# HGRN2's level steps in two-bank score tiles ahead of the projections, its outputs between the attention's units, and the output projection's rows in that order

## The chip, the cores and the metric

The kernel runs on one core of a Trainium2 chip. Its engines work from queues of their own: TensorE (PE in the profile; PEld is its weight load), VectorE (DVE), ScalarE (ACT), GpSimd (POOL) and SyncE (SP), which issues the DMAs here. Semaphores order them against each other. The metric is the device time of one execution in microseconds.

## The reference

One inference step of a two-layer backbone on 384 tokens: 128 context tokens (x_prompt) and 256 latent ones (x_sample), D = 1024, all in fp32. Layer 0 is the one that matters here: windowed attention (A) and a bidirectional HGRN2 (B) share one input projection and one output projection.

```python
def mixer_ab(h, w_in, w_out, sink, lb, gnorm, rope=None, ctx=None):
    qa, ka, va, qb, ib, ff, fb, gb = jnp.split(h @ w_in, EVEN_SPLIT, axis=-1)
    ...
    qb = jax.nn.silu(qb)...
    logf_f, kf = hgrn2_gate(ff, lb[0])      # f = lb + (1-lb)*sigmoid(z); log f, k = 1-f
    logf_b, kb = hgrn2_gate(fb, lb[1])
    ...
    oa = banded_gqa_with_context(rope(qa), rope(ka), va, k_ctx, v_ctx, sink)   # dense_gqa for context
    ob, s_f, s_b = hgrn2_bidir(qb, kf, logf_f, kb, logf_b, ib, s0_f, s0_b)
    ob = rms_norm(ob, gnorm) * jax.nn.silu(gb)
    y = jnp.concatenate([oa, ob], axis=-1) @ w_out
```

HGRN2 is, per head, a state S of 128 x 128 with S <- diag(f_t) S + k_t v_t and output q_t S_t, once forward and once backward, the two added. After the mixer comes x <- LN(alpha*x + gate*y), then a SwiGLU feed-forward; layer 1 (other mixers) follows, and nothing of it is touched.

## The kernel before

A scheduler sets the order of each engine's queue: instructions are taken by the order in which the program writes them, moved by a priority offset. `ahead(part)` sets that offset from the table `AHEAD` for what is written inside it, larger meaning earlier.

*Matmuls.* Activations and weights are split into a high and a low part (hH, hL; wh, wl), and `mm3` (L127 to L129) makes three matmuls of each product. `wload` (L118 to L123) loads a weight into one of three `wr` buffers with a DMA on SP, casts it to wh on ACT (L122) and subtracts on VectorE to get wl (L123). `proj_tm` gives tokens on partitions (tile pj), `proj_fm` features (pf).

*HGRN2.* Four heads in two pairs; a pair has 2 x 384 columns. `hg_proj(pr)` projects q and the two gates f. `hg_levels` builds the matrix AT of decayed scores within 128-token blocks: six diagonal blocks, then seven levels, level lv joining neighbours of m = 2^lv tokens. In each level ACT copies the halves of the scaled keys and queries (Fk, Bk, Fq, Bq) into Kc and Qc (L890 to L893), TensorE makes six score blocks hs (L872) into the one lv bank, four and then two, VectorE merges them into AT under a mask (L911), multiplies the four arrays by products of gates (L900), and forms the next products nB (L907, L908). `hg_out(pr)` then makes states and outputs: transposes tk, products up with the values vB, outputs ho, an rms norm (POOL's rsqrt, L110), the gate gB, transposes ty, and writes rows 4 + 2 pr and 5 + 2 pr of hH and hL.

*Attention.* `attention` is a generator of six steps: the context unit, four pairs of heads, and a last step; step n makes scores and softmax of a unit (s, pr) and then transposes and values of the unit before (pt, ov), which go into rows 0 to 3 of hH and hL.

*Output projection.* `out_first` (in the mixer) projects the first four rows that `ORDER` names onto columns 0 to 511 (o0, o1, o2); `boundary`, written after the mixer, loads the first rows' other columns (out_second, into pools `bndw`), gate gb (L477), x (L480), and the last four rows of w_out, and ends in LN. SP takes its DMAs in the order of its queue, so one that waits holds the rest.

*PSUM.* `open_psum(3, 3, 1)`: three banks for ps (s, pt, tk, up, ho, ty ...), three for pj, one for lv, beside psa's one.

Of the kernel before, what the change touches and what calls it, by code (L numbers as in the profile page):

```python
# [29 lines left out]
AHEAD = {"w": 1500, "w0": -700, "lv0": -30, "lv1": 0, "attA": 400, "attC": 400, "attD": 100, "fin": 500, "qs": -1500,  # L30
         "ada": -400, "ada_step": -500, "of0": -500, "of1": 1500, "ho0": -100, "ho1": -30, "gb": 100, "ib": -60,
# [6 lines left out]
ORDER = ((0, 1, 2, 3, 4, 5, 6, 7), (4, 5, 6, 7, 0, 1, 2, 3))  # L38
# [3 lines left out]
def tile_backbone_step(ctx, tc, I, O):  # L42
# [18 lines left out]
    def lvt(name):  # L61
        return psum["lv"].tile([P, 512], F32, tag="lv", name=name)
# [755 lines left out]
    def mixer_ab():  # L818
# [4 lines left out]
        M = Slots(es, {"one": (1, 0), "pr": (4, 768), "pt": (6, 512), "qS": (2, 1536), "qf": (3, 768),  # L823
                       "X": (8, 768), "at": (2, 768), "vB": (2, 768), "kq": (3, 768), "t2": (5, 512),
# [4 lines left out]
        def hg_tiles():  # L829
            return M.tile("qf", F32), [M.tile("X", F32) for _ in range(4)], [M.tile("qf", F32) for _ in range(2)]  # L830
# [9 lines left out]
        def ev_f(pr, d, X, f):  # L840
            def ev(j, acc):
# [687 lines left out]
```

## Time and profile before

| | us |
|---|---|
| median of three runs | 1096.12 |
| lowest and highest | 1095.95, 1098.69 |
| the profiled execution | 1095.94 |
| its span | 1094.1 |
| TensorE busy in it | 1036.0 |
| VectorE, ACT, POOL busy | 660.6, 440.8, 120.0 |

The span is what the profiler recorded of one execution; what is left of its time lies around it. A row of a timeline gives start and length; one of a group gives busy time, mean of one, and the idle time of the engine before them with what ended it. "hs<-kq" is the operation that writes hs and reads kq; a full-fp32 matmul leaves two records.

### The profile page before, as it was taken

The numbers are of one execution on the slowest core, as the hardware profiler recorded it, in microseconds if no ns is written. First come the engines' busy times: TensorE is split into PE (matmuls) and PEld (weight loads), VectorE is DVE, ScalarE is ACT, GpSimd is POOL, SyncE is SP. The second block draws the span as 40 slices with busy tenths as digits, with TensorE's granted clock in tenths as the row PEclk, the third lists the DMA queues.
The fourth block names the chain that finished last, engine by engine and source line by source line (L and its number), as shares of the span: only waits on it lengthen the run. The fifth ranks groups of instructions, "written<-read, shape, count | busy, mean of one in ns | idle before, by whom it ended". The sixth has DMA issues, their size and how long they took to land. (4 is left out here: it accounts for less than half of the span.)

```text
span 1094.1 us, 15881 instructions
## 1 busy us (share of the span) xinstructions
PE 1036.0 (95%) x6105; PEld 870.7 (80%) x6105; DVE 660.6 (60%) x1140; ACT 440.8 (40%) x804; POOL 120.0 (11%) x166
## 2 busy tenths in 40 slices
PE   5999999987999999999999998979899999999996
PEld 4788767555889999897778786666589999998885
DVE  2575855686598458458236875765489464443237
ACT  2365645363253323232223547545254333332231
POOL 0021201101110000000000343213130000000004
PEclk8999999997999999999999999989999999999998
DMA  9874243484047776766655431144126555543431
GB/s 305 258 222 124 86 142 123 140 275 164 23 150 219 249 221 219 232 210 214 237 190 159 152 108 45 35 150 165 47 79 194 151 172 153 159 135 116 135 116 58
DMA packets 114354, 173.13 MB, mean 158 GB/s; under 512 B 9419, under 2 KB 82150, under 8 KB 114278
## 3 DMA queue, kind: packets, MB, share of 16 engines
q1 hardware_dynamic: 113526, 171.78, 50.0%
q8 instruction: 48, 0.79, 0.3%
q10 hardware_dynamic: 752, 0.34, 0.1%
q14 instruction: 28, 0.23, 0.1%
HBM read 167.84 MB, written 4.24 MB: 157 GB/s over the span
## 5 line engine op out<-in xcount | busy, mean ns | idle before, releaser
L123 DVE TENSOR_TENSOR wl<-wr,wh 128x1024 fp32r<-128x1024 f32 (+4 forms) x200 | 235.7, 1182 | 234.9 <-ACT wh L122 232.3
L122 ACT ACTIVATE wh<-wr 128x1024 fp32r<-128x1024 f32 (+4 forms) x200 | 202.4, 1015 | 347.3 <-PE pf L128 124.0
L127 PE MATMUL pf<-hH,wh 128*128 128x384 f32 x688 | 232.7, 338 | 0.0
L129 PE MATMUL pf<-hH,wl 128*128 128x384 f32 x688 | 232.7, 338 | 0.0
L128 PE MATMUL pf<-hL,wh 128*128 128x384 f32 x688 | 232.6, 338 | 0.0
L129 PEld LDWEIGHTS pf<-hH,wl 128*128 128x128 f32 x688 | 129.4, 188 | 3.1 <-issue 3.1
L128 PEld LDWEIGHTS pf<-hL,wh 128*128 128x128 f32 x688 | 129.4, 188 | 2.7 <-issue 2.6
L127 PEld LDWEIGHTS pf<-hH,wh 128*128 128x128 f32 x688 | 129.4, 188 | 2.3 <-issue 2.2
L128 PE MATMUL o<-wl,aH 128*128 128x512 f32 (+1 forms) x280 | 101.2, 361 | 0.7 <-DVE wl L123 0.7
L127 PE MATMUL o<-wh,aH 128*128 128x512 f32 (+1 forms) x280 | 101.3, 362 | 0.4 <-DVE a L1175 0.4
L129 PE MATMUL o<-wh,aL 128*128 128x512 f32 (+1 forms) x280 | 101.0, 361 | 0.0
L129 PE MATMUL pj<-wh,hL 128*128 128x512 f32 (+3 forms) x240 | 89.0, 371 | 2.0 <-POOL hL L344 1.8
L127 PE MATMUL pj<-wh,hH 128*128 128x512 f32 (+3 forms) x240 | 89.2, 377 | 0.3 <-ACT vA L1106 0.2
L261 DVE SCALAR_TENSOR_TENSOR part<-ar,cT,part 128x512 f32<-128x512 f32 x112 | 80.2, 744 | 15.3 <-DMA ar<-in_w_ada 15.2
L128 PE MATMUL pj<-wl,hH 128*128 128x512 f32 (+3 forms) x240 | 89.0, 371 | 0.0
L110 POOL TENSOR_TENSOR ve<-ve,nhalf 128x1 f32<-128x1 f32 x12 | 7.0, 583 | 617.7 <-DVE ve L530 336.1
L127 PEld LDWEIGHTS o<-wh,aH 128*128 128x128 f32 x280 | 52.9, 189 | 10.2 <-issue 1.4
L128 PEld LDWEIGHTS o<-wl,aH 128*128 128x128 f32 x280 | 52.9, 189 | 9.0 <-DVE wl L123 1.0
L129 PEld LDWEIGHTS o<-wh,aL 128*128 128x128 f32 x280 | 52.8, 188 | 9.2 <-issue 1.2
L129 PEld LDWEIGHTS pj<-wh,hL 128*128 128x128 f32 x240 | 45.1, 188 | 12.2 <-POOL hL L344 2.7
L127 PEld LDWEIGHTS pj<-wh,hH 128*128 128x128 f32 x240 | 44.8, 188 | 10.4 <-issue 2.7
L128 PEld LDWEIGHTS pj<-wl,hH 128*128 128x128 f32 x240 | 45.1, 188 | 8.6 <-issue 1.4
(318 smaller groups left out, 1542.7 us busy)
## 6 DMA issues: line engine op xcount, KB each, us to landing
ar<-in_w_ada SPq DMA_DIRECT2D x80, 512.0 KB
wr<-in_w_ffn_down SPq DMA_DIRECT2D x44, 512.0 KB
wr<-in_w_ffn_gate SPq DMA_DIRECT2D x40, 512.0 KB
wr<-in_w_ffn_up SPq DMA_DIRECT2D x40, 512.0 KB
wr<-in_w_in_ab SPq DMA_DIRECT2D x18, 512.0 KB
ar<-in_w_ada SPq DMA_DIRECT2D x32, 256.0 KB
wr<-in_w_out SPq DMA_DIRECT2D x16, 512.0 KB
wr<-in_w_in_ab SPq DMA_DIRECT2D x16, 256.0 KB
```

What stands on the lines that cost most here:

```text
L110: nc.gpsimd.tensor_tensor(out=out, in0=v, in1=nhalf[:, :n], op=ALU.pow)
L122: nc.scalar.activation(hi, raw, AF.Copy)
L123: nc.vector.tensor_tensor(out=lo, in0=raw, in1=hi.bitcast(F32), op=ALU.subtract)
L127: nc.tensor.matmul(out, lh, rh, start=start, stop=False)
L128: nc.tensor.matmul(out, lh, rl, start=False, stop=False)
L129: nc.tensor.matmul(out, ll, rh, start=False, stop=stop)
L261: nc.vector.scalar_tensor_tensor(out=dst, in0=raw[:, j], scalar=sc, in1=dst, op0=ALU.mult, op1=ALU.add)
```

## The change

It touches five things. The tiles: a pair's keys are one tile X[0] (Fk, Bk), its queries another (Bq, Fq), f is one tile for both directions, so one access covers both halves. `hg_levels`: all six score blocks in one tile of two banks, one merge of 768 columns, one product for the keys, one nB, two copies on ACT. PSUM: `open_psum(2, 3, 1)`, where lv's one buffer now has two banks and ps has two. The program's order: hg_proj(1) and both hg_levels stand before the attention's projections, with new offsets. And the attention's six steps are split, three, then hg_out(0), one, out_first, one, hg_out(1), one, with `ORDER[0]` taking rows 2 and 3 last.

```diff
-AHEAD = {"w": 1500, "w0": -700, "lv0": -30, "lv1": 0, "attA": 400, "attC": 400, "attD": 100, "fin": 500, "qs": -1500,
-         "ada": -400, "ada_step": -500, "of0": -500, "of1": 1500, "ho0": -100, "ho1": -30, "gb": 100, "ib": -60,
+AHEAD = {"w": 1500, "w0": -700, "lv0": 1000, "lv1": 800, "attA": 400, "attC": 400, "attD": 100, "fin": 500, "qs": -1500,
+         "ada": -400, "ada_step": -500, "of0": -500, "of1": 1500, "ho0": 300, "ho1": 300, "gb": 100, "ib": -60,
-ORDER = ((0, 1, 2, 3, 4, 5, 6, 7), (4, 5, 6, 7, 0, 1, 2, 3))
+ORDER = ((0, 1, 4, 5, 6, 7, 2, 3), (4, 5, 6, 7, 0, 1, 2, 3))
...
-        return psum["lv"].tile([P, 512], F32, tag="lv", name=name)
+        return psum["lv"].tile([P, 2, 512], F32, tag="lv", name=name)
...
-        M = Slots(es, {"one": (1, 0), "pr": (4, 768), "pt": (6, 512), "qS": (2, 1536), "qf": (3, 768),
-                       "X": (8, 768), "at": (2, 768), "vB": (2, 768), "kq": (3, 768), "t2": (5, 512),
+        M = Slots(es, {"one": (1, 0), "pr": (4, 768), "pt": (6, 512), "qS": (2, 1536), "f": (1, 1536),
+                       "X": (4, 1664), "at": (2, 768), "vB": (2, 768), "kq": (3, 768), "t2": (5, 512),
...
+        def mixed(X, m):
+            v = X[:, 0:2 * (N2 + m)].rearrange("p (h r) -> p h r", h=2)[:, :, 0:N2]
+            return v.rearrange("p h (g a i) -> p h g a i", a=2, i=m)[:, :, :, 0, :]
...
             def scores(Kc, Qc, take):
-                for b0, nb in ((0, 4), (4, 2)):
-                    pp = lvt("hs").rearrange("p (b t) -> p b t", b=4)
-                    for b in range(nb):
-                        bs = slice((b0 + b) * P, (b0 + b + 1) * P)
-                        nc.tensor.matmul(pp[:, b, :], Kc[:, bs], Qc[:, bs], start=True, stop=True)
-                    take(pp[:, 0:nb, :], slice(b0, b0 + nb), nb)
+                pp = lvt("hs").rearrange("p a (b t) -> p (a b) t", b=4)
+                for b in range(6):
+                    nc.tensor.matmul(pp[:, b, :], Kc(b), Qc(b), start=True, stop=True)
+                take(pp[:, 0:6, :])
...
-                nc.scalar.activation(V(Qc)[:, :, 1, :], V(Fq)[:, :, 1, :], AF.Copy)
-                nc.scalar.activation(V(Qc)[:, :, 0, :], V(Bq)[:, :, 0, :], AF.Copy)
-                nc.scalar.activation(V(Kc)[:, :, 0, :], V(Fk)[:, :, 0, :], AF.Copy)
-                nc.scalar.activation(V(Kc)[:, :, 1, :], V(Bk)[:, :, 1, :], AF.Copy)
+                for c, x in ((Kc, Km), (Qc, Qm)):
+                    nc.scalar.activation(c.rearrange("p (g h i) -> p g h i", h=2, i=m),
+                                         x.rearrange("p h g i -> p g h i"), AF.Copy)
+                scores(blk(Kc), blk(Qc), merge)
...
-                for eng, T, hh, fac in ((nc.vector, Fk, 0, bf[:, :, 1]), (nc.vector, Bk, 1, bb[:, :, 0]),
-                                        (nc.vector, Fq, 1, bf[:, :, 0]), (nc.vector, Bq, 0, bb[:, :, 1])):
-                    eng.tensor_tensor(out=V(T)[:, :, hh, :], in0=V(T)[:, :, hh, :], in1=bc(fac), op=ALU.mult)
+                nc.vector.tensor_tensor(out=Km, in0=Km, in1=bc(kf), op=ALU.mult)
+                nc.vector.tensor_tensor(out=Qm[:, 1], in0=Qm[:, 1], in1=bc(bv[:, 0, :, 0]), op=ALU.mult)
+                nc.vector.tensor_tensor(out=Qm[:, 0], in0=Qm[:, 0], in1=bc(bv[:, 1, :, 1]), op=ALU.mult)
...
-                nc.vector.tensor_tensor(out=nf, in0=bf[:, :, 0], in1=bf[:, :, 1], op=ALU.mult)
-                nc.vector.tensor_tensor(out=nb_, in0=bb[:, :, 0], in1=bb[:, :, 1], op=ALU.mult)
+                nc.vector.tensor_tensor(out=nB, in0=bv[:, :, :, 0], in1=bv[:, :, :, 1], op=ALU.mult)
...
-        ps1 = open_psum(3, 3, 1)
+        ps1 = open_psum(2, 3, 1)
...
         lv0, lv1 = [], []
+        st1 = hg_proj(1)
+        with ahead("lv0"):
+            drain(hg_levels(*st0, lv0))
+        with ahead("lv1"):
+            drain(hg_levels(*st1, lv1))
         a_ctx()
         proj_tm(w, 512, 256, evac_kv)
         proj_tm(w, 0, 512, evac_q)
-        with ahead("lv0"):
-            drain(hg_levels(*st0, lv0))
-        st1 = hg_proj(1)
...
-        with ahead("lv1"):
-            drain(hg_levels(*st1, lv1))
-        with ahead("attA"):
-            drain(attention(M, Att(s_sample, s_prompt, lambda tl, h: vA[:, tl, h // 4, :], 0, SC_A, True)))
+        att = attention(M, Att(s_sample, s_prompt, lambda tl, h: vA[:, tl, h // 4, :], 0, SC_A, True))
+
+        def att_some(n):
+            with ahead("attA"):
+                for _ in range(n):
+                    next(att)
+
+        att_some(3)
         with ahead("ho0"):
             hg_out(0, st0[1], *lv0, vB[0])(gB[:, 0])
+        att_some(1)
         with ahead("of0"):
             first = out_first(I["w_out"][0], ORDER[0])
+        att_some(1)
         with ahead("ho1"):
             hg_out(1, st1[1], *lv1, vB[1])(gB[:, 1])
+        att_some(1)
```

Three places show what moves. First, TensorE's queue around pair 0's first scores (hs). Before (qf is the query of pair 0, pj0 and pj1 accumulators of a projection onto tokens, tk transposes a cached key):

```order
L127 MATMUL pj1_1094<-wh_1083,hH_89 128x512
L128 MATMUL pj1_1094<-wl_1084,hH_89 128x512
L129 MATMUL pj1_1094<-wh_1083,hL_90 128x512
L127 MATMUL pj1_1094<-wh_1110,hH_89 128x512
L872 MATMUL hs_1219<-qf_141,kq_1217 128x128 x4
L794 MATMUL tk_1051<-ident_75,t2_1049 128x128 x2
L128 MATMUL pj0_1087<-wl_1111,hH_89 128x512
L129 MATMUL pj0_1087<-wh_1110,hL_90 128x512
```

and now (pf0 and pf1 belong to hg_proj(1), X_142 holds the query here):

```order
L127 MATMUL pf0_1004<-hH_89,wh_1038 128x384
L128 MATMUL pf0_1004<-hL_90,wh_1038 128x384
L129 MATMUL pf0_1004<-hH_89,wl_1039 128x384
L882 MATMUL hs_1152<-X_142,kq_1150 128x128 x6
L127 MATMUL pf1_1005<-hH_89,wh_1008 128x384
L128 MATMUL pf1_1005<-hL_90,wh_1008 128x384
L129 MATMUL pf1_1005<-hH_89,wl_1009 128x384
L127 MATMUL pf1_1005<-hH_89,wh_1008 128x384
L128 MATMUL pf1_1005<-hL_90,wh_1008 128x384
```

The scores stand among the projections of pair 1's q and f in place of the query's projection, six in one group. Second, TensorE's queue at the end of the mixer. Before, from the last transposes of hg_out(1) (ty) into the output projection (o0, o):

```order
L971 MATMUL ty_2562<-ident_75,kq_2516 128x128 x2
L971 MATMUL ty_2568<-ident_75,kq_2516 128x128 x2
L127 MATMUL o0_2428<-wh_2681,hH_89 128x512
L128 MATMUL o0_2428<-wl_2682,hH_89 128x512
L129 MATMUL o0_2428<-wh_2681,hL_90 128x512
L127 MATMUL o0_2428<-wh_2687,hH_89 128x512
L128 MATMUL o0_2428<-wl_2688,hH_89 128x512
L129 MATMUL o0_2428<-wh_2687,hL_90 128x512
L971 MATMUL ty_2574<-ident_75,kq_2516 128x128
L127 MATMUL o_2641<-wh_2626,hH_89 128x512
```

and now, from the last transposes of hg_out(1) to the output projection, with the last attention unit's transposes (pt) and values (ov) between:

```order
L977 MATMUL ty_2440<-ident_75,kq_2388 128x128 x2
L977 MATMUL ty_2446<-ident_75,kq_2388 128x128 x2
L673 MATMUL pt_2451<-ident_75,pr_2284 128x128 x4
L673 MATMUL pt_2458<-ident_75,pr_2285 128x128 x4
L673 MATMUL pt_2465<-ident_75,pr_2284 128x128 x2
L673 MATMUL pt_2465<-ident_75,pr_2285 128x128 x2
L679 MATMUL ov_2472<-pt_2452,vA_932 64x256
L679 MATMUL ov_2472<-pt_2459,vA_932 64x256
L679 MATMUL ov_2472<-pt_2452,vA_932 64x256
L679 MATMUL ov_2472<-pt_2459,vA_932 64x256
L679 MATMUL ov_2472<-pt_2466,vA_932 64x256 x2
L127 MATMUL o_2543<-wh_2528,hH_89 128x512
```

The last attention unit moved behind hg_out(1), and the first matmul of the rest of the output projection stands behind its values. Third, SP's queue around gb and x. Before (the bracket names the semaphores that a DMA waits for, those of the DMA queues and of engines):

```order
L197 DMA ada_b<-in_b_ada 32x2x128 x3
L118 DMA wr<-in_w_ffn_gate 128x2x256 [waits DMAHW2_49,DMAHW3_49,DMAHW0_49,DVE_49]
L118 DMA wr<-in_w_ffn_up 128x2x256 [waits DMAHW1_49]
L477 DMA gb<-gate_2_805 128x1024 [waits DVE_49,Pool_49]
L477 DMA gb<-gate_2_805 128x1024
L480 DMA x_2599<-in_x_prompt 128x1024 [waits DMAHW4_49]
L480 DMA x_2600<-in_x_sample 128x1024 [waits DMAHW5_49]
L480 DMA x_2601<-in_x_sample 128x1024 [waits DMAHW6_49]
L945 DMA out<-t_2483 128x2x128 [waits DMAHW7_49,Activation_49]
L945 DMA out<-t_2483 128x2x128 [waits DMAHW0_49]
```

and now:

```order
L951 DMA out<-t_2355 128x2x128 [waits Activation_49]
L951 DMA out<-t_2355 128x2x128
L477 DMA gb<-gate_2_801 128x1024 [waits DMAHW3_49,PE_49,Pool_49]
L477 DMA gb<-gate_2_801 128x1024 [waits DMAHW4_49]
L480 DMA x_2501<-in_x_prompt 128x1024 [waits DMAHW5_49]
L480 DMA x_2502<-in_x_sample 128x1024 [waits DMAHW6_49]
L480 DMA x_2503<-in_x_sample 128x1024 [waits DMAHW7_49]
L118 DMA wr<-in_w_out 128x1024 [waits DMAHW0_49,DVE_49]
L118 DMA wr<-in_w_out 128x1024 [waits DMAHW1_49,DVE_49]
L118 DMA wr<-in_w_out 128x1024 [waits DMAHW2_49,DVE_49]
L118 DMA wr<-in_w_ffn_gate 128x2x256 [waits DMAHW3_49,DMAHW0_49,DVE_49]
L118 DMA wr<-in_w_ffn_up 128x2x256 [waits DMAHW4_49]
```

Three rows of w_out, which stood before in front of all these, come right behind x, and gate and up weights behind them; gb waits for TensorE and POOL where it waited for VectorE and POOL.

## Rows read from the trace of the kernel before

**Rows 1.** The page's busy time of each engine, share of the span, instructions.
```profile
PE 1036.0 (95%) x6105; PEld 870.7 (80%) x6105; DVE 660.6 (60%) x1140; ACT 440.8 (40%) x804; POOL 120.0 (11%) x166
```

**Rows 2.** Busy time by stretch: length, engines (instructions), granted clock, DMA share, GB/s.
```profile
58.60:100.00 41.40, 40.41 (x254) 34.45 (x254) 30.24 (x59) 21.92 (x39) 9.48 (x8) 1.00 0.62 184
...
225.00:291.70 66.70, 54.62 (x298) 42.27 (x297) 44.21 (x106) 23.35 (x63) 4.86 (x7) 0.85 0.51 170
58.60:291.70 233.10, 219.89 (x1261) 162.90 (x1261) 152.17 (x323) 112.12 (x237) 32.11 (x39) 0.96 0.47 146
```

**Rows 3.** TensorE's timeline (start, length, line, operation, count): four landmarks.
```profile
58.76 0.36 PE L127 MATMUL pj<-wh,hH 128*128 128x256 f32 x1
...
220.74 0.65 PE L933 MATMUL tk<-ident,X 128*128 128x128 f32 x4
...
251.65 1.11 PE L971 MATMUL ty<-ident,kq 128*128 128x128 f32 x4
...
291.71 0.49 PE L329 MATMUL tp<-ident,x 128*128 128x128 f32 x3
```

**Rows 4.** What TensorE waits for from 55 to 320: total us, times, longest.
```profile
PE hs L872 <- ACT kq L893: 2.6, 3, 1.4
...
PE hs L872 <- DVE at L911: 1.5, 2, 0.8
```

**Rows 5.** TensorE's timeline in hg_out(1) and the output projection.
```profile
256.19 1.06 PE L933 MATMUL tk<-ident,X 128*128 128x128 f32 x4
...
261.98 0.39 PE L953 MATMUL ho<-t,X 128*128 128x128 f32 x2
262.20 0.39 PE L954 MATMUL ho<-t,X 128*128 128x128 f32 x2
...
272.01 0.45 PE L971 MATMUL ty<-ident,kq 128*128 128x128 f32 x1 [0.70 <-DVE kq L968]
...
272.68 0.63 PE L128 MATMUL o<-wl,hH 128*128 128x512 f32 x1
273.11 0.63 PE L129 MATMUL o<-wh,hL 128*128 128x512 f32 x1
...
277.80 0.43 PE L128 MATMUL o<-wl,hH 128*128 128x512 f32 x1
278.07 0.40 PE L129 MATMUL o<-wh,hL 128*128 128x512 f32 x1
278.30 0.39 PE L127 MATMUL o<-wh,hH 128*128 128x512 f32 x1
```

**Rows 6.** Groups by line and shape, 55 to 300: busy us, mean ns; idle time before.
```profile
L123 DVE TENSOR_TENSOR wl<-wr,wh 128x1024 fp32r<-128x1024 f32 x29 | 36.0, 1251 | 14.2 <-ACT wh L122 14.2
L122 ACT ACTIVATE wh<-wr 128x1024 fp32r<-128x1024 f32 x29 | 30.4, 1058 | 26.9 <-PE pj L129 13.3 <-DMA wr<-in_w_ffn_up 4.0 <-PE pf L128 3.4
...
L900 DVE TENSOR_TENSOR X<-X,nB 128x384 f32<-128x384 f32 x48 | 26.2, 576 | 1.0 <-ACT kq L892 0.8
...
L911 DVE COPY_PREDICATED at<-lmask,hs 128x512 f32<-128x512 uint8 x14 | 10.2, 731 | 4.4 <-PE hs L872 4.2
...
L892 ACT ACTIVATE kq<-X 128x384 f32<-128x384 f32 x14 | 7.5, 537 | 11.3 <-PE hs L872 5.6 <-DVE bp L290 3.2 <-issue 1.6
...
L911 DVE COPY_PREDICATED at<-lmask,hs 128x256 f32<-128x256 uint8 x14 | 6.2, 442 | 9.2 <-PE hs L872 9.2
...
L863 DVE TENSOR_TENSOR X<-qf 128x768 f32<-128x768 f32 x2 | 1.9, 952 | 0.0
```

**Rows 7.** SP's timeline (DMA issues) from 155 to 300.
```profile
227.65 0.46 SPq L118 DMA_DIRECT2D wr<-in_w_out  x1
...
256.53 0.82 SPq L477 DMA_DIRECT2D gb<-gate  x2
...
257.87 1.21 SPq L480 DMA_DIRECT2D x<-in_x_sample  x2
```

**Rows 8.** DMA rate of the stretch 225 to 300 in 40 equal slices.
```profile
GB/s 256 323 362 386 389 358 376 297 61 334 266 0 0 161 119 0 0 184 334 365 413 246 10 151 285 128 0 0 0 0 0 0 0 0 34 246 0 9 0 0
```

More of the change, by code (lines that the diff above doesn't have):

```diff
@@ L822, in mixer_ab, with half, hg_tiles @@
         es = ExitStack()
-        M = Slots(es, {"one": (1, 0), "pr": (4, 768), "pt": (6, 512), "qS": (2, 1536), "qf": (3, 768),
-                       "X": (8, 768), "at": (2, 768), "vB": (2, 768), "kq": (3, 768), "t2": (5, 512),
+        M = Slots(es, {"one": (1, 0), "pr": (4, 768), "pt": (6, 512), "qS": (2, 1536), "f": (1, 1536),
+                       "X": (4, 1664), "at": (2, 768), "vB": (2, 768), "kq": (3, 768), "t2": (5, 512),
                        "gB": (1, 1536)})
         gB = M.tile("gB", F32).rearrange("p (a t j v) -> p a t j v", a=2, t=3, j=2)
-        def hg_tiles():
-            return M.tile("qf", F32), [M.tile("X", F32) for _ in range(4)], [M.tile("qf", F32) for _ in range(2)]
+        N2 = 2 * NTOK
+        def half(X, i):
+            return X[:, i * N2:(i + 1) * N2]
+        def mixed(X, m):
+            v = X[:, 0:2 * (N2 + m)].rearrange("p (h r) -> p h r", h=2)[:, :, 0:N2]
+            return v.rearrange("p h (g a i) -> p h g a i", a=2, i=m)[:, :, :, 0, :]
+        def hg_tiles(f):
+            X = [M.tile("X", F32) for _ in range(2)]
+            return half(X[1], 1), X, M.tile(f, F32)
         def ev_q(q):
@@ new lines, in hg_levels, with merge @@
+                G = N2 // (2 * m)
+                Km, Qm = mixed(K, m), mixed(Q, m)
+                def merge(pp):
+                    nc.vector.copy_predicated(AT, C["lmask"][:, lv, :].unsqueeze(1).to_broadcast([P, 6, P]), pp)
+                Kc, Qc = [M.tile("kq", F32) for _ in range(2)]
+                for c, x in ((Kc, Km), (Qc, Qm)):
+                    nc.scalar.activation(c.rearrange("p (g h i) -> p g h i", h=2, i=m),
+                                         x.rearrange("p h g i -> p g h i"), AF.Copy)
@@ L910, in merge @@
-                def merge(pp, bl, nb):
-                    nc.vector.copy_predicated(AT[:, bl, :],
-                                              C["lmask"][:, lv, :].unsqueeze(1).to_broadcast([P, nb, P]), pp)
-                scores(Kc, Qc, merge)
+                    B, W = M.sm.tile([P, N2], F32, tag="nB", bufs=1, name="nB"), NTOK
+                    nB = B.rearrange("p (d g) -> p d g", d=2)
+                else:
+                    nB = bv[:, :, :, 0]
+                nc.vector.tensor_tensor(out=nB, in0=bv[:, :, :, 0], in1=bv[:, :, :, 1], op=ALU.mult)
@@ L1006, in x_turn @@
                     nc.scalar.activation(xT[k // 2][:, k % 2, :], tp[:, :NTOK], AF.Copy)
-        st0 = hg_tiles()
+        st0 = hg_tiles("f")
         acc0 = {}
@@ L1464, in tile_backbone_step @@
             boundary(b1, x_t, l, 0, lambda k: hH[:, k, :], lambda k: hL[:, k, :], ORDER[l], I["w_out"][l], lambda: ms,
-                     x_in if l == 0 else x_mid, False, first, lvt if l == 0 else None, part)
+                     x_in if l == 0 else x_mid, False, first, (lambda name: lvt(name)[:, 0, :]) if l == 0 else None, part)
             with tc.tile_pool(name="part", bufs=1) as pp, tc.tile_pool(name="ffn", bufs=1) as fp:
```

44 lines of the change are left out of this document (18 added, 26 removed).

## The prediction, made before the changed kernel ran

> **What bounds the kernel now.** I read the page first: TensorE is busy for 95% of the span, VectorE for 60% [rows 1]. A change that adds no matmul and takes none away can therefore only move the gaps between TensorE's instructions. Then I looked for the stretch that the change can reach. The two programs give TensorE the same instructions up to the first projection of layer 0 that stands in another place (58.76 us) and again from the first transposes of x behind the output projection (291.71 us) [rows 3]. What lies between takes 232.95 us, and the result is the shift of that second landmark.
>
> How much of it is gap? The table by stretch gives TensorE 219.89 us busy of 233.10 at a mean granted clock of 0.96 [rows 2], but busy time includes the overlap at each start. I priced every matmul by the distance of two starts back to back: 0.23 us for 512 columns, 0.22 for a 128x128 one in full fp32 (two records) [rows 5]; narrower ones in proportion to their columns, the attention's scores at about 1 us a unit. That makes about 193.4 us of pure work, so 39.6 us of gap:
> - 58.76 to 220.74: 147.3 of work in 161.98, gap 14.7, a tenth. Small ones everywhere.
> - 220.74 to 251.65: 18.8 in 30.91, gap 12.1. Here pair 1's level chain runs last, with little beside it: TensorE waits for ACT's copies and VectorE's merges [rows 4], and VectorE has 44.21 us of work in the 66.70 from 225 on [rows 2].
> - 251.65 to 291.71: 27.3 in 40.06, gap 12.8: the second hg_out's serial steps, and the slower clock. [...]
>
> **The change part by part.** *Fewer and wider instructions in a level.* The two merges (731 and 442 ns) become one of 768; the step between the two rows is 289 ns per 256 elements, so about 1020. K's two products become one 768-wide (952 instead of 2 x 576). The Q products stay two. The four ACT copies of 537 become two of about 0.84 (estimated between 537 for 384 and 1058 for 1024). So VectorE saves 0.15 + 0.20 and, for one nB product less, some 0.15: 0.5 us a level, 7 us over 14 levels; ACT 0.44, 6 us [rows 6]. Neither engine is the bound in this range on the whole, so this only shortens a chain where one is exposed. The row shows 202 ns saved by joining two 384-wide products. [...]
>
> *Levels put ahead (front).* hg_proj(1) and all levels now stand before the key, query, v and gate projections. From 58.76 to the seventh group of pair 0's scores I count 49.6 us of TensorE work, with 50.2 of VectorE work: seven level steps, the weights' low parts (1.25 each) and the gates' f and K. VectorE is at 30.24 of 41.40 there now [rows 2]. I take 52.9, a gap of 3.3. From below it could be 1 (the first level's wait only); from above VectorE at nine tenths busy gives 50.2/0.9 = 55.8, gap 6.
>
> *The dense middle.* Up to the first transposes of hg_out(0) there are 80.4 us of work. Before has a gap of a tenth in such a stretch; with VectorE at 62 of 87 I take 8.5%, so 6.8. Bounds 4 (a twentieth) and 9.6 (12%). The scheduler mixes projections, attention units and levels here, so each serial chain has cover.
>
> *hg_out(0) between attention units.* 29.4 us of work. Its steps (tk, up, ho, square, rsqrt on POOL, gate, ty) took 15.9 us in the second hg_out of before, from 256.19 to 272.1 [rows 5]. Now adaLN matmuls and two score units lie beside them; I take 34.6, gap 5.2, bounds 3 and 8.
>
> *The tail.* Order decides here. After the last scores come the transposes and values of the unit before, then the whole of hg_out(1), then transposes and values of the last unit, and nothing else is on TensorE's queue: the remaining output projection waits. hg_out's 15.9 us held ten 512-column matmuls at the slow pitch (4.3), so 11.6 by itself; each unit's transposes, evacuation and values make about 5, the scores 2. [...]
>
> *The output projection's late rows.* In before the last of w_out was issued at 227.65 and gb and x at 256.53 to 259.1, each long before use [rows 7]. In after SP reaches gb only when the last values matmul has released its space (that instant is T0), and then come gb and x (five transfers of 0.52 MB), three rows of w_out (three more) and all gate and up weights. Before, five such transfers took from 256.53 to about 266.3, 9.8 us, by the row of GB/s [rows 8]; three more at its 0.37 MB/us add 4.2. Then a cast (1.06) and a subtraction (1.25) [rows 6]: the last row is usable at T0 + 17. 36 matmuls have other weights and hide in that wait (8.4 us, or 15.4 at the slow pitch). Then 48 x 0.2335 = 11.2, a little of the row in hand, and 2.4 for a clock that rises as late as it did in before, at 277.8 [rows 5]: the landmark is at T0 + 31.2 for 19.6 of work, gap 11.6. Bounds: 5 (eight transfers at 0.40 MB/us, the clock high already) and 18 (all 48 at the slow pitch, +9.3).
>
> Sum of gaps after: 3.3 + 6.8 + 5.2 + 12.4 + 11.6 = 39.3 against 39.6. The profiled execution took 1095.94 us, of which 1.84 lie outside its span of 1094.10; so 1095.94 - 0.3 = 1095.6, and the median of the three runs shown is 0.2 above it. I say 1096. A measurement of this kernel can tell about 0.3%, that is 3.3 us, from no change. If all five terms fell on their bounds together it would be 19.3 us less or 17.3 more; taken as independent, the roots of the summed squares are 9.5 (of 2.3, 2.8, 2.2, 5.4, 6.6) and 8.4 (of 2.7, 2.8, 2.8, 2.6, 6.4).
>
> **The rivals.**
> - *The serial chains really go (faster, 1089).* Pair 1's levels, 12.1 us of gap now, lie under projections, and the tail costs less than I count: if hg_out(1) overlaps with the units before and after it (separate data, the same two banks), 8 of 12.4 remain, and the middle is at a twentieth (4). Sum 32: 7 less. For it speaks that before, hg_out(0) ran beside levels and adaLN without a wait of its own in the list [rows 4]. Against it: two ps banks, and evacuations between.
> - *The clock in the projection (slower, 1103).* TensorE is thin from the last scores to T0 + 17, and the 48 matmuls that follow run at 0.43 instead of 0.23: 9.3 minus the 2.4 I have, +7. It decides if the clock does not rise within the first dozen of them; in before the slow pitch lasted twelve starts, from 272.68 on [rows 5].
> - *The banks (slower, 1101).* The two-bank score tile costs ps one of its three banks, and scores, transposes, values and hg_out's steps share it. If a unit must wait for its evacuation in the dense part the middle's gap goes from 8.5 to 14%: +5. Against it: in before only 1.5 us of TensorE's waits are for the score bank [rows 4], and no other row of that list names an evacuation of a shared bank. [...]
> - That the change doesn't do what it says is excluded by the order of instructions: pair 0's scores do stand between the first projections.
>
> **How the numbers follow.** The cancelling sum 0.38, its own range 1092.5 to 1099; the chains go 0.32; the clock 0.17; the banks 0.13. The likeliest is 1096. The range takes the two roots around it, which holds the other cases' centres as well: 1087 to 1104. Of the first case 0.04 lies beyond 0.3% faster and 0.02 beyond slower: faster 0.36, within 0.3% 0.32, slower 0.32.
>
> **What would show it.** Right: score matmuls among the pf projections from about 70 us on; no waits of hs for kq near the end; an idle TensorE in the tail before the last values matmul; w_out issued right after x, and a TensorE wait of some 9 us for the weights at T0 + 8. Wrong: if the landmark comes before 286, the tail's units overlap or the weights arrive early; if after 297, look for a slow clock in the last 48 matmuls, or for scores and transposes waiting on evacuations between 110 and 200. Everything behind the landmark should keep its lengths; if the feed-forward begins with a wait for its weights, which are now issued behind w_out, I missed that.

## The result: 1.3% slower

The changed kernel takes 1110.95 us (median of 4 runs, 1108.27 to 1115.83) against 1096.03 for the one before, a ratio of 1.013 with a 95% interval of 1.011 to 1.0151. The forecast was 1096, the range 1087 to 1104. Its profiled execution took 1108.27 us with a span of 1106.5, so 12.4 more in the span than before; it was the fastest of the four, so the traces show 12.4 of the 14.9 us between the medians. Two executions far outside all others (2566 us of the kernel before, 3492 us of w2 below) enter no ratio. The page's busy lines of it:

```profile
PE 1037.6 (94%) x6105; PEld 874.2 (79%) x6105; DVE 657.7 (59%) x1094; ACT 434.9 (39%) x772; POOL 114.1 (10%) x166
...
PE   6999999787899999999999998979899999999996
...
PEclk8999999988899999999999999999999999999998
```

TensorE has the 6105 matmuls it had in [rows 1] and is busy for 1.6 us more; the rest of the 12.4 is idle time (at a lower clock the same work counts as busy for longer: in this trace the two score matmuls of a unit for 0.91 us at a granted clock of 1.00, at 219.00, and for 1.65 at 0.50, at 226.44). The thin slices of layer 0 are the eighth to the eleventh (each is 27.7 us, so 194 to 304): busy for 7, 8, 7 and 8 tenths, at a clock of 9, 8, 8 and 8. The landmarks of the prediction, in the timeline of TensorE:

```profile
61.20 0.48 PE L127 MATMUL pf<-hH,wh 128*128 128x384 f32 x1 [2.57 <-DVE vT L174]
...
113.25 1.50 PE L882 MATMUL hs<-kq 128*128 128x128 f32 x12
...
199.94 0.65 PE L939 MATMUL tk<-ident,X 128*128 128x128 f32 x4
...
244.49 0.91 PE L722 MATMUL s<-kT,qS 64*128 64x384 f32 x2
...
268.98 1.17 PE L679 MATMUL ov<-pt,vA 128*64 128x256 f32 x6
...
299.97 1.03 PE L329 MATMUL tp<-ident,x 128*128 128x128 f32 x8
...
303.45 0.39 PE L127 MATMUL o<-wh,hH 128*128 128x256 f32 x1 [2.45 <-DVE x L520]
```

- 61.20: pair 1's first projection waits 2.57 us for vT. In before the first projection there starts at 58.76 [rows 3].
- 113.25: the seventh group of pair 0's scores; forecast 111.7.
- 199.94: the first transposes of hg_out(0); forecast 198.9.
- 244.49: the last unit's scores; forecast 233.5. Here most of it is lost.
- 268.98: the last values matmuls; they end at 270.8. Forecast 260.1, that is 26.6 behind the scores; measured 26.3.
- 299.97: the landmark behind the output projection, 8.3 later than in before (291.71, [rows 3]).
- 303.45: a wait of 2.45 us behind it, where before has none. Sixteen of the matmuls behind it start 0.21 us apart instead of 0.12. Together that is about 4 us, and the time from the landmark to the end of the span is 4.1 longer than in before (806.5 and 802.4).

Busy time by stretch (columns as in [rows 2]), of the kernel before and of the changed one, for the same stretches:

```profile
100.00:190.00 90.00, 90.00 (x469) 64.97 (x468) 56.16 (x110) 51.67 (x103) 12.19 (x16) 1.00 0.38 114
190.00:240.00 50.00, 47.53 (x356) 30.51 (x354) 34.09 (x77) 24.88 (x62) 7.00 (x11) 1.00 0.63 202
240.00:300.00 60.00, 50.26 (x258) 41.12 (x255) 38.97 (x93) 18.87 (x49) 7.08 (x10) 0.83 0.32 105
```

```profile
100.00:190.00 90.00, 90.00 (x535) 68.78 (x534) 65.77 (x107) 49.32 (x91) 11.91 (x16) 1.00 0.45 141
190.00:240.00 50.00, 40.58 (x265) 21.39 (x263) 17.63 (x49) 14.36 (x42) 9.45 (x15) 0.90 0.60 185
240.00:300.00 60.00, 49.09 (x215) 35.08 (x215) 27.28 (x52) 19.62 (x42) 4.95 (x8) 0.86 0.35 119
```

From 100 to 190 both rows have TensorE busy all the time, at full clock. Busy time includes the overlap at each start (from 278.06 on the 512-column matmuls of the changed kernel start 0.23 us apart and are busy for 0.39 or 0.40 each); at the prediction's prices of a matmul the stretch holds some 83 us of work in before and some 87 now (estimates from the counts in the traces). So the change packed it about 4 us tighter, and lost more behind it. VectorE got 9.6 us more of that stretch. From 190 to 240 TensorE is idle for 9.4 us instead of 2.5 and at 0.90 of the clock; VectorE, ACT and DMA have less to do than before too. No engine is busy throughout: each waits for another.

What TensorE waits for from 55 to 330 (answers to [rows 4]):

```profile
PE ada_acc L203 <- DMA ar<-in_w_ada: 5.2, 5, 2.1
PE pt L673 <- ACT pr L643: 3.9, 3, 1.9
PE o L127 <- ACT wh L122: 3.0, 2, 1.8
PE pf L127 <- DVE vT L174: 2.6, 1, 2.6
PE o L127 <- DVE x L520: 2.5, 1, 2.5
```

The waits of hs for copies and merges are gone from the list. In their place stand waits for w_ada, for the softmax (pt for pr), and for the late rows of w_out (o for wh). And the issue of these rows on SP (answers to [rows 7]):

```profile
270.87 0.82 SPq L477 DMA_DIRECT2D gb<-gate  x2
...
272.21 1.13 SPq L480 DMA_DIRECT2D x<-in_x_sample  x2
...
273.45 0.65 SPq L118 DMA_DIRECT2D wr<-in_w_out  x1
...
284.05 0.38 SPq L118 DMA_DIRECT2D wr<-in_w_ffn_gate  x1
```

gb, x and then w_out's three rows are issued as soon as the last values matmul is done, one right behind the other (270.87 to 275.8); the feed-forward's first weights at 284 instead of 232 to 249.

### The profile page after: what moved, and what is told of

Read it like the earlier page. It is cut to its first block, busy times and chain, and to the rows that moved or that the text cites. A ratio compares the mean times of both kernels' runs of the same rounds, so it can differ in the third digit from the quotient of the medians.

```text
span 1106.5 us, 15790 instructions
## 1 busy us (share of the span) xinstructions
PE 1037.6 (94%) x6105; PEld 874.2 (79%) x6105; DVE 657.7 (59%) x1094; ACT 434.9 (39%) x772; POOL 114.1 (10%) x166
## 4 chain that ended last, share of the span: by engine, by line
PE 73%; DVE 10%; DMA 8%; ACT 3%; issue 3%; POOL 2%; SPq 1%; DVEq 0%; ACTq 0%; POOLq 0%
PE pf L127 9%; PE pf L129 9%; PE pf L128 9%; PE o L127 6%; PE o L128 6%; PE o L129 6%; DMA ar<-in_w_ada 5%; PE pj L129 4%; PE pj L127 4%; PE pj L128 3%; PE ada_acc L203 3%; DVE wl L123 2%; PE hs L882 2%; PE s L722 2%; PE ov L679 2%
## 5 line engine op out<-in xcount | busy, mean ns | idle before, releaser
L127 PE MATMUL o<-wh,aH 128*128 128x512 f32 (+1 forms) x280 | 101.3, 362 | 0.4 <-DVE a L1190 0.4
L127 PEld LDWEIGHTS o<-wh,aH 128*128 128x128 f32 x280 | 52.9, 189 | 10.2 <-issue 1.4
L128 PEld LDWEIGHTS o<-wl,aH 128*128 128x128 f32 x280 | 52.9, 189 | 8.7 <-DVE wl L123 0.6
```

Source lines behind the costliest of these rows:

```text
L127: nc.tensor.matmul(out, lh, rh, start=start, stop=False)
L128: nc.tensor.matmul(out, lh, rl, start=False, stop=False)
```

## The experiments

Each kernel ran beside the kernel before on one chip; the table gives the ratio to it with its 95% interval, and from the profiled execution the starts of the first score matmuls, the last values and the transposes of x (the landmark), and the span. The times of a trace are those of one execution. That of f4 is the longest of its ten (1093.39 to 1102.2 us), so its span says less than its ratio.

| kernel | ratio to before | first s | last ov | landmark | span |
|---|---|---|---|---|---|
| before | 1 | 99.2 | 221.3 | 291.7 | 1094.1 |
| changed | 1.013 [1.011, 1.0151] | 138.6 | 269.0 | 300.0 | 1106.5 |
| e1_units_in_a_row | 1.012 [1.0105, 1.0135] | 138.8 | 241.1 | 305.2 | 1106.6 |
| e2_three_ps_banks | 1.0137 [1.012, 1.0153] | 132.7 | 270.9 | 303.9 | 1109.5 |
| e3_levels_rewritten_only | 1.0011 [0.9986, 1.0036] | 101.3 | 230.1 | 290.9 | 1092.0 |
| e4_weave_only | 1.0301 [1.0272, 1.0331] | 99.1 | 284.8 | 315.4 | 1121.2 |
| f1_attention_first | 1.0006 [0.9982, 1.0031] | 101.4 | 233.2 | 289.5 | 1092.8 |
| f3_attention_first_woven | 1.008 [1.0048, 1.0111] | 101.9 | 264.3 | 295.9 | 1102.1 |
| f4_attention_first_levels_high | 1.0008 [0.9984, 1.0032] | 102.7 | 237.6 | 295.7 | 1100.4 |
| w2_last_unit_before_hg_out | 1.0066 [1.0041, 1.009] | 136.6 | 253.7 | 295.3 | 1101.1 |
| d1_filler | 1.0172 [1.0143, 1.0202] | 139.0 | 275.7 | 306.9 | 1113.0 |
| a2_hg_outs_interleaved | 0.9974 [0.9951, 0.9997] | 135.9 | 239.0 | 284.8 | 1090.0 |
| b2_first_and_interleaved | 0.9897 [0.9863, 0.9931] | 101.5 | 233.5 | 278.8 | 1083.9 |
| b3_three_chains | 1.009 [1.0061, 1.0118] | 101.3 | 232.2 | 300.6 | 1106.0 |
| n1_no_ada_loads | 1.0116 [1.0091, 1.0141] | 151.8 | 271.5 | 302.9 | 1109.0 |
| n2_before_no_ada_loads | 1.0011 [0.9993, 1.0028] | 98.0 | 224.0 | 293.8 | 1098.5 |

### Is it the weave, the levels or the banks?

The first theory was W: the weave costs. e1 undoes it alone:

```diff
-ORDER = ((0, 1, 4, 5, 6, 7, 2, 3), (4, 5, 6, 7, 0, 1, 2, 3))
+ORDER = ((0, 1, 2, 3, 4, 5, 6, 7), (4, 5, 6, 7, 0, 1, 2, 3))
...
-        att_some(3)
+        with ahead("attA"):
+            drain(attention(M, Att(s_sample, s_prompt, lambda tl, h: vA[:, tl, h // 4, :], 0, SC_A, True)))
         with ahead("ho0"):
             hg_out(0, st0[1], *lv0, vB[0])(gB[:, 0])
-        att_some(1)
         with ahead("of0"):
             first = out_first(I["w_out"][0], ORDER[0])
-        att_some(1)
         with ahead("ho1"):
             hg_out(1, st1[1], *lv1, vB[1])(gB[:, 1])
-        att_some(1)
```

> The changed kernel with the weave alone undone: the attention's six steps in a row, then hg_out(0), out_first, hg_out(1), and the output projection's rows 0 to 7 in order; levels ahead, two-bank scores, two ps banks and all offsets stay as changed. Theory W (the weave is what costs: the changed kernel's gaps lie in 190 to 271 us, where hg_out and the last units stand in one row with nothing beside them, and in the loads behind the last values): the transposes of x come at about 290 or earlier instead of 299.97, and the kernel takes 1096 to 1100, the rest being the wait of 2.5 us behind the landmark and 2.6 at the first projection, which stay. Rival L (levels ahead cost it): stays within 3 us of 1108 to 1111. Rival P (the missing ps bank makes units and hg_out wait): stays above 1104, with waits on evacuations in 190 to 270.

It stayed at 1.012. W failed as it was put. The loads are indeed no longer late (gb at 241.82 on SP, the last values at 241.1), but the gain is lost again in the stretch from 240 to 300, by stretch in e1:

```profile
190.00:240.00 50.00, 43.19 (x266) 21.91 (x268) 16.43 (x42) 14.20 (x36) 9.65 (x16) 0.90 0.57 174
240.00:300.00 60.00, 43.77 (x194) 34.73 (x191) 27.84 (x60) 18.93 (x48) 4.75 (x7) 0.77 0.38 128
```

TensorE idles for 16.2 of 60 us there and has 0.77 of the clock; there two hg_out follow each other with only parts of the output projection beside them.

e2 gives ps its third bank back and makes the score tile one bank again:

```diff
-        ps1 = open_psum(2, 3, 1)
+        ps1 = open_psum(3, 3, 1)
...
-                pp = lvt("hs").rearrange("p a (b t) -> p (a b) t", b=4)
-                for b in range(6):
-                    nc.tensor.matmul(pp[:, b, :], Kc(b), Qc(b), start=True, stop=True)
-                take(pp[:, 0:6, :])
+                for b0, nb in ((0, 4), (4, 2)):
+                    pp = lvt("hs").rearrange("p (b t) -> p b t", b=4)
+                    for b in range(nb):
+                        nc.tensor.matmul(pp[:, b, :], Kc(b0 + b), Qc(b0 + b), start=True, stop=True)
+                    take(pp[:, 0:nb, :], slice(b0, b0 + nb), nb)
```

> The changed kernel with three ps banks and one score bank: six blocks in two tiles of four and two, merges of 512 and 256; everything else as changed. Theory W: only the wait behind the transposes of x goes (2.5 us and some 1.6 at the slow clock), 4 us less, and the 26 us from the last scores to the last values matmul stay. Rival P: 10 us or more less, the gaps between 190 and 270 shrink.

The time did not move: the bank is not the cause of the loss (rival P, and the prediction's rival of the banks, are out). The 2.45 us behind the landmark are gone from e2's trace, as expected here, but not the 4 us: e2's span behind its landmark is still 3.2 us longer than before's. The wait stands in the traces of the four kernels that have both two ps banks and the late loads (changed, f3, d1, n1: 2.0 to 2.6 us). It is missing in e2 and e4, which have the late loads and three banks, and in e1, e3 and f1, which have two banks and no late loads. In the changed kernel VectorE still subtracts weights (at 288.7, 291.4 and 298.8, 1.23 us each) where LN's steps stand, but it does so in e4 too (305.2, 307.3, 314.7). What the wait costs is not shown: behind the landmark the sixteen traces take 801.1 to 806.5 us, and w2, without the wait, takes 805.8.

e3 is the level code with its tiles and banks in the old order and with the old offsets, e4 the weave, its row order and the hg_out offsets in the kernel before:

```diff
-        with ahead("attA"):
-            drain(attention(M, Att(s_sample, s_prompt, lambda tl, h: vA[:, tl, h // 4, :], 0, SC_A, True)))
+        att = attention(M, Att(s_sample, s_prompt, lambda tl, h: vA[:, tl, h // 4, :], 0, SC_A, True))
+        att_some(3)
         with ahead("ho0"):
             hg_out(0, st0[1], *lv0, vB[0])(gB[:, 0])
+        att_some(1)
...
```

> The kernel before with the level code, the tiles and the banks of the changed one, in the old program order with the old offsets and rows. Theory W: near before, at most the 4 us of the ps bank slower and a few us of the shorter level chain faster, 1092 to 1100. Rival P: 1100 or more. Rival L says nothing of it.

> The kernel before with the weave, its row order and the two offsets of hg_out, and nothing of the levels. Theory W: slower than before by 8 us or more, 1104 and up, with a thin TensorE in the last 40 us ahead of the transposes of x and w_out's rows issued behind x. Rivals L and P: within 3 us of before.

The level code alone changes nothing that can be measured. The weave alone costs 3.0%, in a kernel where the attention starts early: it puts the fourth and fifth unit behind hg_out(0) and the fifth's values behind hg_out(1), and these wait for pair 0's and pair 1's levels, which are late there (last values at 284.8 instead of 221.3). So both parts of the order cost time by themselves, and together no more than the levels ahead alone (e1, where the attention is late).

### Is it the late attention?

In e1, slower than before and without the weave, the first scores stand at 139 instead of 99. Theory F: the attention's projections wait behind hg_proj(1) and the levels, the levels' and projections' matmuls, which could lie beside the units' softmax and beside hg_out, are used up, and what is left is a row of serial chains. By it f1 was to be back at before, at 1094 to 1099. f1 is e1 with the attention's projections first and the level offsets at 0, f4 the same with the offsets 1000 and 800, f3 as f1 with the weave:

```diff
-AHEAD = {"w": 1500, "w0": -700, "lv0": 1000, "lv1": 800, "attA": 400, "attC": 400, "attD": 100, "fin": 500, "qs": -1500,
+AHEAD = {"w": 1500, "w0": -700, "lv0": 0, "lv1": 0, "attA": 400, "attC": 400, "attD": 100, "fin": 500, "qs": -1500,
...
+        a_ctx()
+        proj_tm(w, 512, 256, evac_kv)
+        proj_tm(w, 0, 512, evac_q)
         st1 = hg_proj(1)
         with ahead("lv0"):
             drain(hg_levels(*st0, lv0))
         with ahead("lv1"):
             drain(hg_levels(*st1, lv1))
-        a_ctx()
-        proj_tm(w, 512, 256, evac_kv)
-        proj_tm(w, 0, 512, evac_q)
```

> The kernel of e1_units_in_a_row (no weave) with the key, value and query projections written ahead of hg_proj(1) and the levels, and the level offsets at 0: the attention's first scores then stand behind 42 us of TensorE work as in before (39), not behind 75, and the level groups spread on to 147. [...] Rival T (it is the two ps banks and the casts of w_out's rows in hg_out's way that make the late stretch slow): stays at 1105 or more, since both are unchanged.

> As f1_attention_first (no weave, the attention's projections written first), but with the level offsets of the changed kernel, 1000 and 800: first scores behind 43 us of work as in f1, last level group at 129 instead of 147. Theory F2 (it is the late start of the attention's own projections that costs, not early levels): within 3 us of f1, 1094 to 1100. Rival L2 (early levels, which take the cover away from units and hg_out): 1105 or more, nearer to e1 at 1109.5.

> The same order of projections and levels with the weave of the changed kernel kept. Theory F: the weave itself has its price here, since with early scores the units that it holds back (the fourth and fifth) could have run under levels: 1102 to 1112, slower than f1 by 6 or more. Rival W2 (the weave is harmless, the late attention alone costs): within 3 us of f1.

f1 and f4 are back at before. f4 differs from e1 in nothing but the place of the attention's projections, and its levels are nearly as early (the last level's score matmuls start at 192 us; 182 in e1, 214 in f1), so early levels by themselves do no harm (rival L2 is out): without the weave it is the attention's start. f3 is 0.8% slower, so the weave has its own price of about 8 us here as well, and W2 is out. Of the two parts of the order, the late attention and the weave, each keeps most of the loss when the other alone is undone (e1 1.012, f3 1.008); without both the kernel is at before.

How the late start costs its 12 us is not shown. Theory F's cover does not tell e1 from f4: from the last values to the landmark both run the same 207 matmuls, nearly all of the two hg_out and the output projection. The attention's end comes only 3.5 us later in e1 (241.1 against 237.6), though its start comes 36 later. The rest is in that stretch, which took 64.1 us at a clock of 0.79 in e1 and 58.1 at 0.85 in f4 (their rows stand with a2 and b2 below).

### What the serial end is worth

w2 keeps the changed order, but the attention's last step comes ahead of hg_out(1):

```diff
-ORDER = ((0, 1, 4, 5, 6, 7, 2, 3), (4, 5, 6, 7, 0, 1, 2, 3))
+ORDER = ((0, 1, 4, 5, 2, 3, 6, 7), (4, 5, 6, 7, 0, 1, 2, 3))
...
-        att_some(1)
+        att_some(2)
         with ahead("ho1"):
             hg_out(1, st1[1], *lv1, vB[1])(gB[:, 1])
-        att_some(1)
```

> The changed kernel with the attention's last step moved ahead of hg_out(1), rows of the output projection 0, 1, 4, 5, 2, 3, 6, 7. What waits for the last values matmul (gb, x, three rows of w_out, the casts) then runs beside hg_out(1). If the late loads cost what the trace shows behind T0 (9.5 us of gap in 29.1): 5 to 8 less than the changed kernel, 1103 to 1106. If hg_out(1) then stands as bare as the unit did: within 3 of 1111.

It gains 0.6% on the changed kernel, some 7 us, within what was expected from the late loads, and the wait behind the landmark is gone from its trace.

d1 adds work to the changed kernel instead of moving any:

```diff
+        def fill(n):
+            with tc.high_priority(offset=-600):
+                dm = lvt("dm")
+                for i in range(n):
+                    nc.tensor.matmul(dm[:, 0, 0:256], C["identR"], C["bmask"].rearrange("p a b -> p (a b)"), start=True, stop=True)
+
         att_some(3)
+        fill(40)
...
             first = out_first(I["w_out"][0], ORDER[0])
+        fill(40)
```

> The changed kernel with 80 additional matmuls of 256 columns on constants (0.11 us each, 8.8 us of TensorE work that nothing reads), 40 written behind the third attention step and 40 behind out_first, at low priority. Theory F: they lie in gaps and hold the clock up, the kernel grows by 3 us or less. If TensorE's queue were the bound there: 8 to 9 more, 1119 to 1120.

The ratio rose from 1.013 to 1.0172, 4.6 us for 8.8 us of work: between the two forecasts, and with both intervals taken together anything from about 1 to 8, so it decides little. In the trace all 80 lie from 190.1 to 215.4. The first forty stand ahead of hg_out(0), which starts 4.1 us later (204.03); the other forty stand beside it, and from there to the last unit's scores it takes 2.4 us more. They did not hold the clock up: it is at 0.50 from 230 to 242.

a2 and b2 run the two hg_out side by side, written as generators that take turns; the second has its states in the tile f, its transposed keys in pt slots, and its accumulators in the score bank, which is free by then. out_first stands behind both. a2 does this to e1, b2 to f1, and b3 to f1 with hg_out(0) beside the attention's last two steps and hg_out(1) alone:

```diff
-        def hg_out(pr, X, AT, eb, vB):
+        def hg_out(pr, X, AT, eb, vB, gB, bank, other):
...
+                yield
+                up = bank("up").rearrange("p (i d) -> p i d", i=4)
-                up = pst("up").rearrange("p (i d) -> p i d", i=4)
...
-            hg_out(0, st0[1], *lv0, vB[0])(gB[:, 0])
+            drain(hg_out(0, st0[1], *lv0, vB[0], gB[:, 0], pst, False),
+                  hg_out(1, st1[1], *lv1, vB[1], gB[:, 1], lambda name: lvt(name)[:, 0, :], True))
         with ahead("of0"):
             first = out_first(I["w_out"][0], ORDER[0])
-        with ahead("ho1"):
-            hg_out(1, st1[1], *lv1, vB[1])(gB[:, 1])
```

> As e1_units_in_a_row (levels ahead, attention late, no weave), with the two hg_out written step by step in turn, the second with tiles and a score bank of its own, ahead of out_first. If the bare serial chains at the end are what e1 pays for (some 29 us of gap from 240 to 290): two chains side by side take 8 to 12 off, 1098 to 1102. If TensorE there waits for VectorE's casts or the bank: within 3 of 1109.5.

> As f1_attention_first with the two hg_out in turn as in a2. Theory F: the gap of 20 us from 220 to 270 in f1 shrinks by 6 to 10, 1087 to 1092, better than before and after. If not: 1095 to 1099.

> As b2, but hg_out(0) runs in turn with the attention's last two steps (with a score bank of its own), and hg_out(1) behind them alone. Theory F: half of b2's gain, 1090 to 1095, since one chain stands bare at the end.

a2 takes 16 us off e1 (0.9974 against 1.012), and b2 is 1.0% faster than before, at 1085.45 us (median of 6 runs) the best kernel of the study. Both gained more than was expected of them. The stretch from the last values to the landmark, in e1, f4, a2 and b2:

```profile
241.08:305.15 64.07, 47.84 (x207) 38.29 (x207) 31.83 (x66) 18.93 (x48) 4.75 (x7) 0.79 0.39 127
```

```profile
237.58:295.67 58.09, 44.35 (x207) 34.72 (x207) 29.91 (x63) 19.21 (x48) 4.77 (x7) 0.85 0.40 138
```

```profile
238.99:284.77 45.78, 36.31 (x195) 29.68 (x195) 29.99 (x62) 18.10 (x47) 4.89 (x7) 0.96 0.52 167
```

```profile
233.54:278.83 45.29, 36.27 (x196) 29.50 (x196) 30.03 (x62) 18.13 (x47) 4.87 (x7) 0.96 0.51 169
```

With nearly the same matmuls a2 takes 45.8 us where e1 takes 64.1. TensorE is idle for 9.5 us instead of 16.2, and the clock is 0.96 instead of 0.79: one chain fills the other's waits. b3 shows the counterpart. Both hg_out of it use the one score bank, hg_out(1) stands alone at the end, and the landmark moves to 300.6. From TensorE's waits:

```profile
PE ho L961 <- DVE kq L974: 7.3, 3, 2.6
PE ty L981 <- DVE kq L974: 4.1, 2, 2.6
```

I had expected a gain of it. With one bank for a whole chain, ho and ty wait for VectorE's reading of the tile before; how much of the loss is the bank and how much the chain that stands alone, b3 does not tell apart.

### The waits for w_ada

The list of waits names w_ada first, with 5.2 us. In n1 and n2 each adaLN chunk loads one of its eight blocks and uses it eight times:

```diff
-        for k in range(KD):
-            raw = adap.tile([P, 2, 512], F32, tag="ar", name="ar")
-            dma(out=raw, in_=I["w_ada"][l, k * P:(k + 1) * P, c * D:(c + 1) * D].rearrange("p (h n) -> p h n", h=2))
+        raw = adap.tile([P, 2, 512], F32, tag="ar", name="ar")
+        dma(out=raw, in_=I["w_ada"][l, 0:P, c * D:(c + 1) * D].rearrange("p (h n) -> p h n", h=2))
+        for k in range(KD):
             ada_mm(acc, cTv[:, k, :], raw, k == 0, k == KD - 1)
```

> The changed kernel with seven of eight loads of each adaLN chunk of layer 0's mixer left out: a chunk loads its first block of w_ada and uses it eight times, so the modulation is another and its matmuls never wait for a load but the first. If the waits for w_ada are what made the stretch from hg_out(0) to the last scores longer than forecast: 6 to 9 less than the changed kernel, 1102 to 1105 (5.2 of waits and some clock). If the chains are bare anyway and the waits only fill the time of the chains: within 3 of 1111.

> The kernel before with the same loads left out, as control: its list shows 1.5 us of such waits, so 1 to 3 less than before, 1094 to 1096.

n1 stayed at 1.0116, though in it the DMA engines are at a share of 0.09 from 190 to 271, and the other waits come up instead:

```profile
190.00:271.00 81.00, 67.19 (x395) 41.24 (x395) 27.93 (x81) 25.06 (x77) 13.90 (x22) 0.86 0.09 27
```

```profile
PE pt L673 <- ACT pr L643: 3.4, 2, 1.7
...
PE s L722 <- ACT pr L643: 1.6, 1, 1.6
```

TensorE is still idle for 13.8 of the 81 us, with 0.86 of the clock. It isn't a clean removal: the scheduler put the adaLN matmuls ahead of hg_out(0), whose first transposes come at 209.7 instead of 199.9, and the last unit's scores come at 245.7, not at 244.5. From the one to the other n1 has

```profile
209.68:245.72 36.04, 29.69 (x137) 18.71 (x135) 13.08 (x39) 10.48 (x35) 4.45 (x7) 0.86 0.10 31
```

with no adaLN matmul in it. TensorE is idle for 6.35 us there, against 7.35 in the changed kernel, where 5.2 are waits for w_ada. So these waits for the most part filled time that the chains took anyway. n2, the control, stayed at before (1.0011), where 1 to 3 us less were expected.

## Why the prediction was wrong

- **The front and the middle.** 52.9 and 87.2 us were forecast (work and gap added), ending at 198.9 with the first transposes of hg_out(0). Measured were 54.5 up to the seventh group of scores and 86.7 from there, ending at 199.9. Both terms were right, but not every part of the front: it holds the 2.57 us wait for vT. I had taken the order up to 58.76 as fixed and didn't ask what pair 1's projection would wait for, when it took the place of another at the head.
- **hg_out(0) between the units: the step that failed.** 34.6 us were forecast with bounds 32.4 and 37.4, a gap of 5.2 with bounds 3 and 8; measured 44.55 (199.94 to 244.49), a gap of 15 over the 29.4 of work, which the counts in the trace bear out (29.6). I priced hg_out's steps as the chain and the units and adaLN matmuls beside it as cover. In the trace the units are a chain of their own, scores, softmax, transposes, values, and adaLN's matmuls wait themselves. TensorE runs thin, and the clock falls, in the stretch as a whole and in the timeline of the changed kernel:

```profile
199.94:244.49 44.55, 37.20 (x228) 20.61 (x226) 13.81 (x42) 10.26 (x35) 4.39 (x7) 0.89 0.54 163
```

```profile
219.00 0.91 PE L722 MATMUL s<-kT,qS 64*128 64x384 f32 x2
...
221.23 0.91 PE L722 MATMUL s<-kT,qS 64*128 64x384 f32 x2 [0.22 <-DVE hL L133]
...
222.72 0.64 PE L203 MATMUL ada_acc<-ar,cT 128*32 128x256 f32 x8 [0.33 <-DMA ar<-in_w_ada]
...
225.43 1.08 PE L203 MATMUL ada_acc<-ar,cT 128*32 128x256 f32 x8 [2.07 <-DMA ar<-in_w_ada]
...
226.44 1.65 PE L722 MATMUL s<-kT,qS 64*128 64x384 f32 x2
...
228.42 1.65 PE L722 MATMUL s<-kT,qS 64*128 64x384 f32 x2
```

  The two score matmuls of a unit take 0.91 us at 219.00 and 1.65 at 226.44: the granted clock is 1.00 over the one and 0.50 over the other, and waits of 0.33 and 2.07 us lie between them. Of the 15 us, TensorE is idle for 7.35. The granted clock is 0.50 from 225.2 to 235.2; the matmuls that start there are 4.5 us of work at full clock, so the clock costs about as much again (an estimate from their counts). Some 3 us lie in the starts. So the clock, which the sum had only in other terms, makes up nearly half of the miss of 10 us. How the idle time divides between hg_out's chain and the units' stays open; without adaLN's matmuls and their waits it is 6.35 (n1).
- **The tail.** 26.6 forecast from the last scores to the last values' end, 26.3 measured, in part by luck. The serial sum of hg_out(1) and two units was right, and the clock fell in it (0.50 from 250 to 252, 0.55 from 266 to 268), but hg_out(1) took 13.0 us (253.10 to 266.12), at a mean granted clock of 1.00, where 11.6 was taken. The forecast was that serial sum, 23.6, and 3 us for the clock, which makes the gap of 12.4 over 14.2 of work. The 3 us were my estimate, and no run shows them as a term of their own; the runs show the two falls of the clock above and 1.4 us more for hg_out(1), so about half of the 3 us went there.
- **The output projection's late rows.** 31.2 forecast, 29.1 measured (270.87 to 299.97); gb, x and w_out's rows queue up as forecast, and undoing it in w2 gives about 7 us. The parts differ. Instead of one wait of some 9 us at T0 + 8 there are two of 1.2 and 0.8 at the start and two of 1.8 and 0.8 at T0 + 12 (282.82 and 284.08), with 27 matmuls ahead of these and 57 behind. Twelve of the 57 start at the slow pitch (0.43 us apart from 284.68 to 289.37, at a granted clock of 0.50; 0.23 apart from 290.17 on, at 1.00), as in before.
- **Behind the landmark.** I forecast no change; it was 4.1 us. I asked there only for the feed-forward's weights, not for the steps of LN on VectorE (x, L520), for which TensorE waits 2.45 us. Whether that wait is the 4.1 is not shown (see e2).
- **The level code.** Copies of 768 took 910 ns where I estimated 0.84 us, the merge 1034 ns for 1020, the K product 954 for 952 [rows 6]:

```profile
L905 ACT ACTIVATE kq<-X 128x768 f32<-128x768 f32 x28 | 24.3, 910 | 23.9 <-PE hs L882 16.3 <-issue 4.3 <-DVE rope L1235 3.3
...
L901 DVE COPY_PREDICATED at<-lmask,hs 128x768 f32<-128x768 uint8 x14 | 14.5, 1034 | 9.0 <-PE hs L882 9.0
L912 DVE TENSOR_TENSOR X<-X,nB 128x768 f32<-128x768 f32 x12 | 11.5, 954 | 0.4
```

  The sizes were right, the copies' up to 8%, and the whole rewrite is worth nothing that can be measured (e3). With 954 ns measured for 768 columns and 554 to 587 for 384, a join saves some 187 ns (twice their middle, 570.5, less 954), where I took 202 (200 by the means in [rows 6]).
- **The rivals.** "The serial chains really go" was the most likely of them, and the opposite of what happened: the change left more of them bare. The clock rival has a part in it, in another place. The landmark came after 297, and neither place named for that case holds the loss: the late rows took 2.1 us less than forecast, and from 110 to 200 TensorE has a single wait, 1.9 us of pt for the softmax. The banks rival is out by e2: two ps banks instead of three had no measurable price here (1.013 for the changed kernel, 1.0137 for e2); where one bank serves a whole chain (b3), ho and ty wait for VectorE, 7.3 and 4.1 us.
- **What the account left out altogether.** I added up the gaps stretch by stretch with each stretch's own cover, but never asked what the moved work had covered where it was. Pair 1's levels were in before the work beside the attention's end and hg_out(0); the attention's projections, pushed back by 36 us of TensorE work, moved the start of the attention's chain from 99 to 139. f4 puts only that back in e1, which has no weave, and is at before again. In the woven kernel putting it back (f3, with the level offsets at 0) leaves 0.8%. So two steps of the order failed, not one, and that the lost cover is the reason is argued, not shown.

## What to carry to other kernels

When independent work is moved ahead of a serial chain, cost the chain at its new start, and the place that the work leaves: the sum of busy time stays (TensorE: 1036.0 us before, 1037.6 after), so what is won in a dense stretch (4 us here) can be lost in a thin one. Here starting the attention first paid (f4 against e1), and so did letting the two hg_out take turns with tiles and banks of their own (b2: 1.0% faster than before), while weaving hg_out between attention units that end later cost (f3 against f1). A wait that is first in the list may for the most part fill a chain's time; leaving its cause out (n1) is a way to ask, if one looks where the work went.

## What was not expected of the hardware

- TensorE's granted clock fell from 1.00 to 0.50 at about 225 and was back at about 235, in a stretch that was busy for eight tenths (190 to 240: 40.58 of 50, mean clock 0.90), and it fell three more times up to 277. Two score matmuls took 0.91 us at the one clock and 1.65 at the other, so that this thin stretch cost more than its waits. In e1 the mean was 0.77 over 60 us.
- 8.8 us of additional independent matmuls ahead of that stretch and in its first part did not keep it from falling (d1: 0.50 from 230 to 242).
